# Mixer C's units of a hybrid encoder: other PSUM banks, other queueing, and A's outputs transposed at other jobs

## The chip, the cores and the metric

The kernel runs on one core of a Trainium2 chip. The metric is device microseconds of that core. One execution of the kernel before was also profiled; its times below come from that one.

## The reference, cut to what matters

Two layers work on 256 tokens of width 1024. Per layer, one projection of the normalised input gives queries, keys and values of four attention mixers A, B, C, D, and four gates. Each mixer's output goes through its own branch matrix, is gated, and the sum goes through an output matrix; then a gated feed-forward part with a three-tap convolution follows.

```python
aq, ak, av, bq, bk, bv, cq, ck, cv, dq, dk, dv, g = split_parts(h @ w_in[l])
o_a = diff_attention(aq, ak, av, lam[l], subln_g[l], lambda_init)   # 4 heads, two softmaxes each, then RMSNorm
o_c = dilated_attention(cq, ck, cv)   # 8 heads; windows with dilations 1, 4, 16, joined by their denominators
merged = sum(gate[:, :, i] * (o_i @ w_branch[l, i]))    # i over A, B, C, D
x = x + merged @ w_out[l]
x = x + conv_ffn(rms_norm(x, norm2_g[l]), ...)
```

## The kernel before, in words

**Jobs.** All large matrices stream through the core as jobs. A job is 1 MB of weights: it is loaded (three jobs ahead), each half is split into a high part (`hi`, a cast on ACT, L281) and a low part (`lo`, a subtraction on DVE, L285), and PE multiplies with three passes: high by high (L338), low weights by high (L339), high weights by low (L340). A job of a projection is 24 products of 128 x 512. `ORDER` lists the projections of a layer: `qA` is the queries of mixer A, `gA0` the first half of gate A, `bA0` the first half of A's branch matrix, and so on. A projection of 1024 rows takes two jobs, a branch half one.

**Attention units.** Between the products of the jobs stand the attention units. `UNITS` gives for each mixer the job at which its first unit is handed in and the distance of the next ones (C: job 37, then every 1.5 jobs). A unit of C is two heads of one tile of 128 queries; there are 4 for each of 2 tiles. `go(i)` hands in, at one point, the steps of three neighbouring units: the transposes of unit i-1's probabilities (`transp`, L542, each followed by a copy to SBUF on ACT, L647), the multiplication of unit i-2's probabilities by the values (`pv`, L538) and unit i's scores (`score`, L538). The scores of C are two whole-array matmuls for each head (the dense window) and eight 64 x 64 ones (the dilated groups). Mask and row minimum run on DVE (L576), the exponential on ACT (L577), the reciprocal on DVE (L579), the scaling on ACT (L582).

**Order.** Within the handed-in program a list scheduler with its own timeline decides in which order the instructions stand on each engine, subject to data, buffers and explicit edges: `behind` puts an instruction behind named ones. `mma` and `tra` chain a unit's PE instructions one behind the other, through `self.chain`, which is empty at the start of a `go`. `self.last_mm` is the last product of a job so far. On each engine the instructions run in the order in which they stand.

**PSUM.** Eight banks: four under the tag `mm` for products, three under `ts` for transposes and scores, one under `o`. C's outputs of a tile's four units gather in the `o` bank (L701 in `pv`) and leave it at once after the last unit (`evac_split`: a cast on ACT, L442, then a subtraction on DVE, L448).

**A's outputs.** `finish` scales and normalises A's outputs of a tile (DVE L719, ACT L721 for squares, DVE L723, two POOL instructions, DVE L725). `o_transpose` (L737) transposes them and splits them into two tiles of its own from `o_tiles`; it is handed in one job before `bA0`. The tiles `qs` hold the queries of a mixer, split into a high and a low part; they are free once the last scores are done. Mixer B already writes its outputs there.

Of the kernel before, what the change touches and what calls it, by code (L numbers as in the profile page):

```python
# [11 lines left out]
F32R = mybir.dt.float32r  # L12
# [5 lines left out]
S = 256  # L18
# [64 lines left out]

UNITS = {MD: (11, 1.75), MB: (9.75, 1.1), MA: (22.75, 1.1), MC: (37, 1.5)}


class Trunk:
# [465 lines left out]

    def score(self, u):

# [4 lines left out]
        if m == MC:  # L560

            ps, es = [self.ps("ts") for i in range(2)], [self.etile() for i in range(2)]
            u["e"] = es
            self.dense_score(ps[0][:, :256], st, 2 * k, t)
            for g in (1, 2):
                for b in range(2):
                    bs = slice(t * 128 + 64 * b, t * 128 + 64 * b + 64)
                    c0 = 256 + 64 * ((g - 1) if b == 0 else (2 - g))
                    for i in (1, 0):
                        r = slice(64 * i, 64 * i + 64)  # L570
                        self.mma(ps[i][64 * b:64 * b + 64, c0:c0 + 64], st["qT"][g][r, k, bs], st["kT"][g][r, k, bs], start=True, stop=True)
            self.dense_score(ps[1][:, :256], st, 2 * k + 1, t)
            mn = self.small("mn", 8)
# [75 lines left out]
    def pv(self, u):  # L649
# [33 lines left out]
        if m == MD:  # L683
# [7 lines left out]
            w = lambda x: x.rearrange("p k (u t s j) -> p t s k u j", u=4, t=2, s=2)[:, t]  # L691
            oh, ol = (w(x) for x in self.o_tiles(st))
            self.evac_split([(pv[:, s], oh[:, s], ol[:, s]) for s in range(2)])
            return
        if k == 0:
            st["o"] = self.ps("o")
        o = st["o"]
        for i in range(3):
            for b in range(1 if i < 2 else 2):

                w = slice(0, 128) if i < 2 else slice(64 * b, 64 * b + 64)  # L701
                for a in range(2):
                    hs = slice((2 * k + a) * 64, (2 * k + a) * 64 + 64)
                    self.mma(o[64 * a:64 * a + 64, k * 128 + w.start:k * 128 + w.stop], v[0][:, i, hs] if i < 2 else v[1 + t][:, b, hs],
                             u["pt"][a][:, i * 128 + w.start:i * 128 + w.stop], start=i == 0, stop=i == 2 and b == 1)
        if u["last"]:
            self.evac_split([(four(o), *(half(x, t) for x in self.o_tiles(st)))])

# [17 lines left out]

    def o_tiles(self, st):
        if "oT" not in st:
            st["oT"] = [self.t4([128, 4, S], F32R) for i in range(2)]
        return st["oT"]  # L730

    def o_transpose(self, st, m, t):
        if m != MA:
            return
        p = self.ps("ts")
        for i in range(4):
            self.nc.tensor.transpose(p[:, i * 128:(i + 1) * 128], st["osb"][:, t, i * 128:(i + 1) * 128], self.ident)  # L737
        self.evac_split([(four(p), *(half(x, t) for x in self.o_tiles(st)))], scale=st["scale"][:, 0:1])


    def layer(self, l):
# [182 lines left out]
        def units(m, s0, step):  # L924
# [5 lines left out]
            def go(i):  # L930
                self.chain = None
                steps = ((i - 1, lambda u: self.transp(u, 0)), (i - 2, self.pv), (i - 1, lambda u: self.transp(u, 1)), (i, self.score))
                for j, f in steps:
                    if 0 <= j < len(us):
                        f(us[j])

# [8 lines left out]
        for what in ORDER.split():  # L945
# [10 lines left out]
            elif kind == "v":  # L956
                vblock(i, (AV, None, CV, DV)[i] + c * 512, c)
            elif kind == "g":
                gate(i, c)
                if i not in seen:  # L960
                    for t in range(2):
                        self.at(J(slot[0] - 1), t, lambda i=i, t=t: self.o_transpose(stt[i], i, t))
            else:
                branch(i, c, seen <= {i})
# [6 lines left out]
        for i, (s0, step) in UNITS.items():  # L971
            units(i, s0, step)
        ns = slot[0]

# [326 lines left out]
```

## Time and profile before

| | |
|---|---|
| median of 3 runs (lowest to highest) | 1230.11 us (1229.86 to 1231.45) |
| the profiled execution's own time | 1229.92 us |
| its span | 1228.1 us |
| PE busy | 1205.8 us, 98% |
| DVE, ACT, POOL busy | 889.7, 729.9, 124.2 us |

Times in the profile run from the span's start. A line such as L338 is a line of the kernel before; PE is the matrix engine, DVE the vector engine, ACT the scalar engine. The span starts a little after the execution's begin and ends a little before its end, so 1.8 us lie around it.

### The profile page before, as it was taken

What the parts mean: (1) busy time and instruction counts of PE and PEld (TensorE: products, weight loads), DVE (VectorE), ACT (ScalarE), POOL (GpSimd) and SP (SyncE); (2) the same over time, 40 slices, a digit from 0 to 9 for tenths busy, and PEclk for the clock granted to TensorE, in tenths of its full rate; (3) what the DMA queues carried; (4) which work ended last, traced back from release to release, by engine and by line L of the source; (5) the groups of instructions that cost most, each with busy time, mean ns of one, the idle gap of its engine ahead of it and who ended that gap; (6) DMA issues with size and microseconds to landing.
All of it is one profiled execution on the core that took longest, in us unless ns stands there. A gap on an engine that the chain in (4) does not pass through costs nothing.

```text
span 1228.1 us, 18650 instructions
## 1 busy us (share of the span) xinstructions
PE 1205.8 (98%) x7325; PEld 1031.0 (84%) x7325; DVE 889.7 (72%) x1431; ACT 729.9 (59%) x1219; POOL 124.2 (10%) x88
## 2 busy tenths in 40 slices
PE   8999999999899999999999999999998999999998
PEld 6887788888778899998878878788886888999986
DVE  6898876975446598886488978769664566888853
ACT  4557666566654466665365676755756545666641
POOL 0331130310000000000023202113000000000000
PEclk9999999999899999999999999999999999999999
DMA  8757346544455465565544754556353453655651
GB/s 261 247 166 234 122 161 199 172 171 144 148 140 172 137 201 178 178 217 175 203 169 157 208 187 142 172 167 204 106 184 110 147 196 104 235 178 173 199 180 66
DMA packets 127670, 212.08 MB, mean 173 GB/s; under 512 B 9085, under 2 KB 56797, under 8 KB 127582
## 3 DMA queue, kind: packets, MB, share of 16 engines
q1 hardware_dynamic: 125836, 205.90, 50.5%
q0 software_dynamic: 1280, 4.20, 1.5%
q8 instruction: 58, 0.95, 0.3%
q10 hardware_dynamic: 466, 0.79, 0.2%
q14 instruction: 30, 0.25, 0.1%
HBM read 203.53 MB, written 1.05 MB: 167 GB/s over the span
## 4 chain that ended last, share of the span: by engine, by line
PE 94%; ACT 3%; DVE 2%; DMA 0%; issue 0%; POOL 0%; SPq 0%; DVEq 0%; ACTq 0%; POOLq 0%
PE mm L338 18%; PE mm L340 18%; PE mm L339 18%; PE mm L336 7%; PE mm L335 7%; PE mm L334 7%; PE ts L538 3%; PE ts L340 2%; PE ts L339 2%; PE ts L338 2%; PE o L538 2%; PE ts L542 2%; PE ts L508 1%; PE o L340 1%; PE o L338 1%; PE o L339 1%
## 5 line engine op out<-in xcount | busy, mean ns | idle before, releaser
L285 DVE TENSOR_TENSOR lo<-w,hi 128x1024 fp32r<-128x1024 f32 x376 | 456.8, 1223 | 207.9 <-ACT hi L281 207.0
L281 ACT CAST hi<-w 128x1024 fp32r<-128x1024 f32 x376 | 392.6, 1049 | 296.4 <-PE mm L340 171.7
L338 PE MATMUL mm<-hi,hTh 128*128 128x512 f32 (+1 forms) x796 | 310.4, 391 | 1.7 <-DVE qn L495 0.5
L339 PE MATMUL mm<-lo,hTh 128*128 128x512 f32 (+1 forms) x796 | 308.6, 388 | 0.4 <-DVE lo L285 0.4
L340 PE MATMUL mm<-hi,hTl 128*128 128x512 f32 (+1 forms) x796 | 307.3, 388 | 0.0
L336 PE MATMUL mm<-hTl,hi 128*128 128x256 f32 x672 | 190.2, 283 | 0.0
L335 PE MATMUL mm<-hTh,lo 128*128 128x256 f32 x672 | 190.2, 283 | 0.0
L334 PE MATMUL mm<-hTh,hi 128*128 128x256 f32 x672 | 189.9, 283 | 0.0
L338 PEld LDWEIGHTS mm<-hi,hTh 128*128 128x128 f32 x796 | 149.7, 188 | 34.4 <-issue 2.2
L339 PEld LDWEIGHTS mm<-lo,hTh 128*128 128x128 f32 x796 | 149.7, 188 | 30.3 <-issue 1.5
L340 PEld LDWEIGHTS mm<-hi,hTl 128*128 128x128 f32 x796 | 149.7, 188 | 29.9 <-DVE hTl L448 0.9
L336 PEld LDWEIGHTS mm<-hTl,hi 128*128 128x128 f32 x672 | 129.1, 192 | 0.0
L335 PEld LDWEIGHTS mm<-hTh,lo 128*128 128x128 f32 x672 | 129.1, 192 | 0.0
L334 PEld LDWEIGHTS mm<-hTh,hi 128*128 128x128 f32 x672 | 128.9, 192 | 0.0
L338 PE MATMUL mm<-hi,t 128*128 128x512 f32 (+1 forms) x192 | 74.2, 387 | 4.1 <-ACT t L442 4.1
L160 POOL TENSOR_TENSOR sm_qr<-sm_qr,mhalf 128x16 f32<-128x16 f32 (+1 forms) x24 | 77.5, 3228 | 2.0
L340 PE MATMUL mm<-hi,t 128*128 128x512 f32 (+1 forms) x192 | 73.6, 384 | 0.0
L339 PE MATMUL mm<-lo,t 128*128 128x512 f32 (+1 forms) x192 | 73.3, 382 | 0.0
L1103 ACT ACTIVATE e<-mm,cwT 128x256 f32<-128x256 f32 x88 | 47.1, 561 | 30.9 <-PE mm L336 29.8
L406 POOL TENSOR_TENSOR sm_nr<-sm_nr,mhalf 128x1 f32<-128x1 f32 x8 | 4.4, 550 | 502.6 <-DVE sm_nr L403 493.8
L159 POOL TENSOR_SCALAR sm_qr<-sm_qr 128x16 f32<-128x16 f32 (+1 forms) x24 | 25.7, 1073 | 283.1 <-DVE sm_qr L497 283.0
L538 PE MATMUL ts<-t,t 64*64 64x64 f32 (+2 forms) x576 | 51.9, 274 | 0.3
(164 smaller groups left out, 1603.5 us busy)
## 6 DMA issues: line engine op xcount, KB each, us to landing
w<-in_w_in_dram SPq DMA_DIRECT2D x97, 1024.0 KB, 4.9
w<-in_w_up_dram SPq DMA_DIRECT2D x44, 1024.0 KB, 4.9
w<-in_w_down_dram SPq DMA_DIRECT2D x22, 1024.0 KB, 4.8
w<-in_w_branch_dram SPq DMA_DIRECT2D x16, 1024.0 KB, 4.9
w<-in_w_out_dram SPq DMA_DIRECT2D x8, 1024.0 KB, 4.9
t<-t POOLq DMA_DIRECT2D x16, 256.0 KB, 4.7
t<-t SPq DMA_DIRECT2D x32, 64.0 KB, 2.0
t<-in_rpb_dram SPq DMA_DIRECT2D x32, 62.5 KB, 5.1
```

The source lines that it names most:

```text
L159: nc.gpsimd.tensor_scalar(dst, ss, EPS, None, op0=ALU.add)
L160: nc.gpsimd.tensor_tensor(dst, dst, mh, ALU.pow)
L281: self.nc.scalar.copy(hi, w)
L285: self.last_split = self.nc.vector.tensor_tensor(lo, w, hi[:].bitcast(F32), ALU.subtract).ins
L334: mm(out, wh, xh, start=first, stop=False)
L335: mm(out, wl, xh, start=False, stop=False)
L336: mm(out, wh, xl, start=False, stop=last)
L338: mm(out, xh, wh, start=first, stop=False)
L339: mm(out, xh, wl, start=False, stop=False)
L340: self.last_mm = mm(out, xl, wh, start=False, stop=last).ins
L538: self.chain = (self.nc.tensor.matmul(out, stationary, moving, **kw).ins,)
L1103: nc.scalar.activation(y[:, b:b + 256], o[:, b:b + 256], AF.Identity, scale=cw(1, z), bias=cw(3, z))
```

## The change

1. `score` for C takes two banks of which the second is the `o` bank. The first (`u["bank"]`) is a `ts` bank that unit i shares with the outputs of unit i-2: scores in columns 0 to 383, outputs in 384 to 511. The 64 x 64 scores come first, then the dense ones.
2. `pv` of C returns a function that splits the unit's outputs; it is called behind the next scores. The outputs go to the place of C's queries (`qs`), unit by unit.
3. `go` starts its chain at `self.last_mm`, and hands in the two transposes first, then the multiplication, then the scores.
4. A's outputs are transposed at jobs 33 and 38 (`OUT_A`) and written to the place of A's queries. `o_tiles` is gone; only D keeps output tiles of its own.

On PE, in layer 1, where the kernel before scores its fifth unit of C and then transposes it: `ts` and `o` are PSUM banks, `e` probabilities, `pt` transposed probabilities. Before:

```order
L538 MATMUL ts_2990<-t_497_2548,t_473_2414 64x64
L538 MATMUL ts_2989<-t_497_2548,t_473_2414 64x64
L538 MATMUL ts_2990<-t_328_1735,t_448_2284 128x256
L538 MATMUL ts_2990<-t_330_1737,t_448_2284 128x256
L542 MATMUL ts_3069<-ident,e_2991 128x128 x3
L538 MATMUL o_2770<-pt_2969,t_400_2068 64x128
L538 MATMUL o_2770<-pt_2983,t_400_2068 64x128
```

The transposes of `e_2991` stand directly behind the last scores of the same unit. After (its line numbers are higher by 2 to 7; L341 to L343 are the three products), at a unit of C:

```order
L342 MATMUL mm_3358<-lo_3268,hTh 128x512
L343 MATMUL mm_3358<-hi_3267,hTl 128x512
L341 MATMUL mm_3359<-hi_3267,hTh 128x512
L342 MATMUL mm_3359<-lo_3268,hTh 128x512
L545 MATMUL ts_3194<-ident,e_3110 128x128 x3
L545 MATMUL ts_3200<-ident,e_3111 128x128 x3
L541 MATMUL ts_3193<-pt_3090,t_400_2068 64x128
L541 MATMUL ts_3193<-pt_3096,t_400_2068 64x128
L541 MATMUL ts_3193<-pt_3090,t_400_2068 64x128
```

The six transposes stand behind 37 products counted from the unit before, and the multiplication follows both groups.

On PE, at A's output transposes of layer 1 (`t_408_2099` holds A's normalised outputs). Before, tile 0, in front of the first products of A's branch matrix:

```order
L538 MATMUL ts_3094<-t_328_1735,t_448_2284 128x256
L538 MATMUL ts_3094<-t_330_1737,t_448_2284 128x256
L737 MATMUL ts_3176<-ident,t_408_2099 128x128 x4
L338 MATMUL mm_3269<-hi_3148,t_626_3181 128x512
L339 MATMUL mm_3269<-lo_3149,t_626_3181 128x512
L542 MATMUL ts_3185<-ident,e_3095 128x128 x3
```

After, tile 0, between A's last multiplication (`o_2229`) and the head transposes of C (L511):

```order
L343 MATMUL mm_2593<-hi_2588,hTl 128x512
L541 MATMUL o_2229<-t_242_1301,pt_2310 128x128 x4
L739 MATMUL ts_2427<-ident,t_408_2099 128x128 x4
L511 MATMUL ts_2556<-ident,qn_2481 128x128 x4
L511 MATMUL ts_2562<-ident,qn_2481 128x128 x4
L341 MATMUL mm_2736<-hi_2632,hTh 128x512
L342 MATMUL mm_2736<-lo_2633,hTh 128x512
```

The branch products that read the result come some ten jobs later; those of `mm_2736` that now follow the head transposes are of another projection.

On ACT, at the same place (`mm_2496`, `mm_2497`, `mm_2503`, `mm_2504` are product banks with C's values). Before:

```order
L281 CAST hi_2736<-w_2641 128x1024
L532 COPY t_497_2548<-ts_2549 128x4x128
L838 COPY t_500_2573<-mm_2496 64x512 x2
L838 COPY t_501_2574<-mm_2497 64x512 x2
L838 COPY t_500_2573<-mm_2585 64x512
L721 ACTIVATE o_2229<-t_408_2099 128x512
L838 COPY t_500_2573<-mm_2585 64x512
```

After:

```order
L284 CAST hi_2750<-w_2648 128x1024
L445 ACTIVATE t_231_1232<-ts_2427,sg_163 128x4x128
L728 ACTIVATE o_2229<-t_408_2099 128x512
L535 COPY t_498_2555<-ts_2556 128x4x128
L840 COPY t_501_2580<-mm_2503 64x512 x2
L840 COPY t_502_2581<-mm_2504 64x512 x2
L840 COPY t_501_2580<-mm_2592 64x512 x2
```

The copy of A's transposed outputs (L445) is new there, and the squares of `finish` (L721, now L728) moved from behind five copies of C's values to in front of them.

```diff
--- before.py
+++ after.py
@@ -82,6 +82,9 @@
 ORDER = "qD kB kD qB kA vD qA vA gD0 kC1 kC0 qC1 bD0 gD1 vC0 qC0 qC2 bD1 kC2 vC1 vC2 gB0 bB0 gB1 bB1 gA0 bA0 gA1 bA1 gC0 bC0 gC1 bC1"
 
 UNITS = {MD: (11, 1.75), MB: (9.75, 1.1), MA: (22.75, 1.1), MC: (37, 1.5)}
+
+
+OUT_A = (33, 38)
 
 
 class Trunk:
@@ -551,7 +554,7 @@
     def etile(self):
         return self.sb(self.tp, "e", [128, 512], F32, bufs=4)
 
-    def score(self, u):
+    def score(self, u, out=None):
 
         nc = self.nc
         m, t, k, st = u["m"], u["t"], u["k"], u["st"]
@@ -559,9 +562,8 @@
         st["sums"][t] = sums
         if m == MC:
 
-            ps, es = [self.ps("ts") for i in range(2)], [self.etile() for i in range(2)]
+            ps, es = [u.get("bank") or self.ps("ts"), self.ps("o")], [self.etile() for i in range(2)]
             u["e"] = es
-            self.dense_score(ps[0][:, :256], st, 2 * k, t)
             for g in (1, 2):
                 for b in range(2):
                     bs = slice(t * 128 + 64 * b, t * 128 + 64 * b + 64)
@@ -569,7 +571,10 @@
                     for i in (1, 0):
                         r = slice(64 * i, 64 * i + 64)
                         self.mma(ps[i][64 * b:64 * b + 64, c0:c0 + 64], st["qT"][g][r, k, bs], st["kT"][g][r, k, bs], start=True, stop=True)
-            self.dense_score(ps[1][:, :256], st, 2 * k + 1, t)
+            for i in range(2):
+                self.dense_score(ps[i][:, :256], st, 2 * k + i, t)
+            if out:
+                out()
             mn = self.small("mn", 8)
             for i in range(2):
                 e, h = es[i][:, :384], 2 * k + i
@@ -689,22 +694,24 @@
                         self.mma(o[64 * a:64 * a + 64, c], v[1 + t][:, s, h * 64:h * 64 + 64], u["pt"][a][:, c], start=True, stop=True)
             pv = o.rearrange("p (k s u j) -> p s k u j", k=4, s=2, u=4)
             w = lambda x: x.rearrange("p k (u t s j) -> p t s k u j", u=4, t=2, s=2)[:, t]
-            oh, ol = (w(x) for x in self.o_tiles(st))
+            if t == 0:
+                st["oT"] = [self.t4([128, 4, S], F32R) for i in range(2)]
+            oh, ol = (w(x) for x in st["oT"])
             self.evac_split([(pv[:, s], oh[:, s], ol[:, s]) for s in range(2)])
             return
-        if k == 0:
-            st["o"] = self.ps("o")
-        o = st["o"]
+
+        o = u.get("bank") or self.ps("ts")
         for i in range(3):
             for b in range(1 if i < 2 else 2):
 
                 w = slice(0, 128) if i < 2 else slice(64 * b, 64 * b + 64)
                 for a in range(2):
                     hs = slice((2 * k + a) * 64, (2 * k + a) * 64 + 64)
-                    self.mma(o[64 * a:64 * a + 64, k * 128 + w.start:k * 128 + w.stop], v[0][:, i, hs] if i < 2 else v[1 + t][:, b, hs],
+                    self.mma(o[64 * a:64 * a + 64, 384 + w.start:384 + w.stop], v[0][:, i, hs] if i < 2 else v[1 + t][:, b, hs],
                              u["pt"][a][:, i * 128 + w.start:i * 128 + w.stop], start=i == 0, stop=i == 2 and b == 1)
-        if u["last"]:
-            self.evac_split([(four(o), *(half(x, t) for x in self.o_tiles(st)))])
+
+        st["oT"] = st["qs"]
+        return lambda: self.evac_split([(o[:, 384:], *(half(x, t)[:, k] for x in st["oT"]))])
 
     def finish(self, u, o):
 
@@ -724,18 +731,13 @@
         self.rsqrt_mean(rr[:, :4], rr[:, :4], 4)
         nc.vector.tensor_tensor(hv(osb), hv(osb), rr.unsqueeze(2).to_broadcast([128, 4, 128]), ALU.mult)
 
-    def o_tiles(self, st):
-        if "oT" not in st:
-            st["oT"] = [self.t4([128, 4, S], F32R) for i in range(2)]
-        return st["oT"]
-
-    def o_transpose(self, st, m, t):
-        if m != MA:
-            return
+    def o_transpose(self, st, t):
+
+        st["oT"] = st["qs"]
         p = self.ps("ts")
         for i in range(4):
             self.nc.tensor.transpose(p[:, i * 128:(i + 1) * 128], st["osb"][:, t, i * 128:(i + 1) * 128], self.ident)
-        self.evac_split([(four(p), *(half(x, t) for x in self.o_tiles(st)))], scale=st["scale"][:, 0:1])
+        self.evac_split([(four(p), *(half(x, t) for x in st["oT"]))], scale=st["scale"][:, 0:1])
 
 
     def layer(self, l):
@@ -928,11 +930,20 @@
             us = [{"m": m, "t": t, "k": k, "st": stt[m], "l": l, "last": k == n - 1} for t in range(2) for k in range(n)]
 
             def go(i):
-                self.chain = None
-                steps = ((i - 1, lambda u: self.transp(u, 0)), (i - 2, self.pv), (i - 1, lambda u: self.transp(u, 1)), (i, self.score))
-                for j, f in steps:
-                    if 0 <= j < len(us):
-                        f(us[j])
+
+                self.chain = (self.last_mm,)
+                out = None
+                if m == MC and 2 <= i < len(us):
+                    us[i - 2]["bank"] = us[i]["bank"] = self.ps("ts")
+                if 1 <= i <= len(us):
+                    for j in range(2):
+                        self.transp(us[i - 1], j)
+                if i >= 2:
+                    out = self.pv(us[i - 2])
+                if i < len(us):
+                    self.score(us[i], out)
+                elif out:
+                    out()
 
             for i in range(len(us) + 2):
                 self.fat(J(s0 + i * step), lambda i=i: go(i))
@@ -957,9 +968,6 @@
                 vblock(i, (AV, None, CV, DV)[i] + c * 512, c)
             elif kind == "g":
                 gate(i, c)
-                if i not in seen:
-                    for t in range(2):
-                        self.at(J(slot[0] - 1), t, lambda i=i, t=t: self.o_transpose(stt[i], i, t))
             else:
                 branch(i, c, seen <= {i})
             if kind == "b":
@@ -970,6 +978,8 @@
         self.at(J(20), -1, scale_a)
         for i, (s0, step) in UNITS.items():
             units(i, s0, step)
+        for t, j in enumerate(OUT_A):
+            self.at(J(j), 1, lambda t=t: self.o_transpose(stt[MA], t))
         ns = slot[0]
```

## Rows read from the trace of the kernel before

**Rows 1.** The page: engines (busy, share, instructions), and the chain's shares by engine.

```profile
PE 1205.8 (98%) x7325; PEld 1031.0 (84%) x7325; DVE 889.7 (72%) x1431; ACT 729.9 (59%) x1219; POOL 124.2 (10%) x88
...
PE 94%; ACT 3%; DVE 2%; DMA 0%; issue 0%; POOL 0%; SPq 0%; DVEq 0%; ACTq 0%; POOLq 0%
```

**Rows 2.** PE's waits over the run: total, times, longest, in us.

```profile
PE ts L542 <- ACT e L582: 5.3, 2, 2.6
PE mm L338 <- ACT t L442: 4.1, 4, 1.4
```

**Rows 3.** Stages: length, busy time by engine, granted clock (PEclk), DMA share, GB/s.

```profile
324.00:331.00 7.00, 4.21 (x49) 3.26 (x48) 3.24 (x7) 5.05 (x11) 0.00 (x0) 0.91 0.45 152
331.00:338.00 7.00, 5.88 (x47) 4.69 (x47) 2.22 (x7) 4.05 (x10) 0.00 (x0) 0.60 0.21 76
930.00:937.00 7.00, 4.21 (x52) 3.17 (x52) 2.79 (x7) 5.37 (x12) 0.00 (x0) 1.00 0.44 150
937.00:943.00 6.00, 4.60 (x45) 3.76 (x43) 2.45 (x7) 3.95 (x10) 0.00 (x0) 0.72 0.28 87
```

**Rows 4.** Timeline of PE, layer 1, 322 to 344: start, length, idle before.

```profile
322.39 0.39 PE L338 MATMUL mm<-hi,hTh 128*128 128x512 f32 x1
...
322.61 0.39 PE L339 MATMUL mm<-lo,hTh 128*128 128x512 f32 x1
...
325.11 0.49 PE L542 MATMUL ts<-ident,e 128*128 128x128 f32 x3
...
325.53 0.89 PE L538 MATMUL o<-pt,t 128*64 128x128 f32 x16
...
330.81 0.90 PE L542 MATMUL ts<-ident,e 128*128 128x128 f32 x3 [2.65 <-ACT e L582]
...
331.64 1.55 PE L538 MATMUL o<-pt,t 128*64 128x128 f32 x16
...
335.61 1.05 PE L737 MATMUL ts<-ident,t 128*128 128x128 f32 x4
...
337.79 0.50 PE L338 MATMUL mm<-hi,t 128*128 128x512 f32 x1 [1.12 <-ACT t L442]
...
338.13 0.40 PE L339 MATMUL mm<-lo,t 128*128 128x512 f32 x1
...
343.43 0.60 PE L737 MATMUL ts<-ident,t 128*128 128x128 f32 x4
```

**Rows 5.** Timeline of PE and ACT, layer 1, 269 to 275.

```profile
269.90 1.04 PE L508 MATMUL ts<-ident,qn 128*128 128x128 f32 x8
...
270.69 0.48 PE L340 MATMUL mm<-hi,hTl 128*128 128x512 f32 x1
...
271.89 1.04 PE L508 MATMUL ts<-ident,qn 128*128 128x128 f32 x8
...
272.69 1.38 PE L538 MATMUL ts<-t,t 128*128 128x256 f32 x20
...
273.01 2.97 ACT L838 COPY t<-mm 64x512 f32<-64x512 f32 x5
...
274.24 0.50 PE L338 MATMUL mm<-hi,hTh 128*128 128x512 f32 x1 [0.17 <-ACT t L838]
```

**Rows 6.** Timeline of DVE and ACT, a softmax of C, layer 1.

```profile
342.06 0.56 DVE L576 CUSTOM_DVE_ANT_0 e<-ts,maskc 128x384 f32<-128x384 f32 x1 [3.54 <-PE ts L538]
...
344.65 1.11 ACT L582 ACTIVATE e<-e,sm_cf 128x384 f32<-128x384 f32 x2
```

**Rows 7.** Groups by line: busy, mean ns; idle before, who released it.

```profile
L281 ACT CAST hi<-w 128x1024 fp32r<-128x1024 f32 x376 | 392.6, 1049 | 296.4 <-PE mm L340 171.7 <-PE o L340 58.6 <-PE mm L336 48.5
...
L448 DVE TENSOR_TENSOR t<-o,t 128x256 fp32r<-128x256 f32 (+1 forms) x20 | 9.1, 472 | 9.1 <-ACT t L442 9.1
...
L442 ACT CAST t<-o 128x256 fp32r<-128x256 f32 (+1 forms) x20 | 7.9, 419 | 2.1 <-PE o L538 2.1
...
L442 ACT ACTIVATE t<-ts,sg 128x512 fp32r<-128x512 f32 x4 | 2.7, 677 | 0.2
```

## The prediction

> **What bounds the kernel now.** I read the page's engine shares and its chain first. The matrix engine PE is busy for 98% of the span and carries 94% of the chain [rows 1]. So only two things can shorten the run: time in which PE waits or runs slowly, and time that PE loses when it changes between kinds of work. Vector (DVE, 72%) and scalar (ACT, 59%) matter only where PE waits for them.
>
> The list of PE's waits comes next. Two sorts lie where the change works [rows 2]. The transposes of mixer C's probabilities wait for the softmax, 5.3 us in 2 waits. The first products of A's branch matrix wait for the copies of A's transposed outputs, 4.1 us in 4 waits. Both occur once in each layer's stage, at 324 to 345 us and at 930 to 950 us.
>
> The table by stage then shows a second loss at the same place: the granted clock. It is 0.91 in 324 to 331 us and 0.60 in 331 to 338 us, so 0.09 x 2 x 7 + 0.40 x 2 x 7 = 6.9 us passed at 1.2 GHz instead of 2.4. In layer 2 it is 1.00 and then 0.72 of 6 us, so 3.4 us [rows 3]. Before it fell, PE had stood idle for 2.65 us in either layer (5.3 over 2).
>
> The timeline shows why [rows 4]. At 325.11 a C unit is transposed and its successor multiplied and scored, all without products between. The next transposes need the softmax of the unit just scored and start only at 330.81. From there on the same groups take 0.90 instead of 0.49 us (three transposes), 1.55 instead of 0.89 (16 passes of probabilities by values) and 1.05 instead of 0.60 (A's four transposes). A's transposes start at 335.61, and the first product on their result at 337.79.
>
> **The change part by part, in us over both layers.**
>
> 1. *C's units queued behind products.* In the order after, 31 to 41 products stand between one unit's scores and its transposes; before, two units of a layer had none or two. The 5.3 of waiting goes. What is late next is the softmax itself. At 342.06 its first reduction starts and its second scaling ends at 344.65 + 1.11 = 345.76 [rows 6], a chain of 3.7 us. The cover is at least 31 x 0.23 (322.39 to 322.61 is one product's pitch [rows 4]) = 7 us, mostly 8.4. With one high-part cast of 1.05 in ACT's way [rows 7] and one low part on DVE of the same order, the chain is some 6 us. I take no wait.
>
> 2. *A's outputs transposed at jobs 33 and 38.* Their first reader is now some ten jobs away. The 4.1 goes.
>
> 3. *Tails of those six waits.* A wait is counted from the end of the last pass, but PE normally starts the next before that: transposes that began at 269.90 end at 270.94, and the product behind them starts at 270.69 [rows 5], 0.25 earlier. So 6 x 0.25 = 1.5 more.
>
> 4. *The half clock.* The three pairs of groups above sum to 3.50 against 1.98, a factor of 1.77. The work from 330.81 to 336.66 (5.85 us) would have taken 3.3, a loss of 2.5. Layer 2's 3.4 us by the same factor lose 1.5. Sum 4.0, gone with the wait that precedes it.
>
> 5. *Fewer changes of kind.* Counting in both orders, between the same two places of a layer, each step from one kind of PE work to another (products, transposes, whole-array scores, 64 x 64 scores, probabilities by values): 71 before, 54 after. One change costs about 0.11: the product at 337.79 is followed after 0.34 [rows 4], not 0.23. 17 x 2 x 0.11 = 3.7. Bounds: 0, if the skipped changes are the cheap ones, and 7, if each costs twice that.
>
> 6. *The new wait.* This is the dear part. A's first transposes (tile 0) now stand in front of C's head transposes, and on ACT their copy and the squares of A's normalisation (L721) stand in front of the copies L838 that free a product bank. Before, PE already waited there, 0.17 us at 274.24, for the second of those copies (they run from 273.01 at 0.6 each [rows 5]). After, 0.68 (A's copy [rows 7]) and 0.6 (the squares) come first, which puts the second copy's end at about 274.2 + 1.25 = 275.45. PE is there sooner, because the scores that it did at 272.69 now come behind those products. From 271.89 it has A's 4 and 8 head transposes; 8 took 0.80 there from start to start (to 272.69), so 12 take 1.2 and it could go on at 273.1. It stands 2.3, and the 0.17 with its tail of 0.25 is gone: 2 x (2.3 - 0.4) = 3.8 added. Bounds: 0 (ACT catches up) and 3.0 a layer (one more cast in front).
>
> 7. *The clock after the new wait.* The rows have the clock fall after gaps of 2.65 and not after one of 1.1 (335.61 + 1.05 to 337.79; at 343.43 A's transposes take 0.60 again [rows 4]). The new gap is 2.3 less a tail, 2.1, nearer to 2.65, so I let it fall once in each layer, at the price of layer 2's stretch: 2 x 1.5 = 3.0. Bounds 0 and 5. The Trainium skill, in "TensorE: Matmul & The Clock Gate" (HAM oscillation), lets the clock drop only after idle gaps longer than any of these. By that rule this term is 0 and the sum 3.0 lower; the trace does not agree, as 2.65 was enough.
>
> 8. *Evacuations unit by unit.* C's outputs leave in 8 pieces of 128 x 128 a layer instead of 2 of 128 x 512, so 12 more copies on ACT and 12 more subtractions on DVE over the run. A 128 x 256 piece takes 0.42 and 0.47 [rows 7]; smaller ones no more. That is 5.0 and 5.7 us at most on engines that are busy for 59 and 72% [rows 1], so nothing on PE. Without that cover they delay a softmax by 0.9, inside the 1 to 2.4 us that term 1 leaves. The wait that the shared bank adds (the outputs leave after the next scores) holds up only that copy and the mask behind it.
>
> 9. *The end.* The last unit's outputs are multiplied later, during gate C and its branch product. The order has the products of the next gate step in front of those that need them: 17 to 20 products, 3.9 us, behind the multiplication, against 0.9 for copy and subtraction. No wait. Nothing changes from the first merge transposes on. The new tile places (four fewer tiles a layer) take away waits of loads, if anything, and no PE wait is on a load there.
>
> **Sum.** Removed 5.3 + 4.1 + 1.5 + 4.0 + 3.7 = 18.6; added 3.8 + 3.0 = 6.8; net 11.8 less. The profiled execution took 1229.92 us (span 1228.1), so 1218.1, and since the median of the runs shown is 1230.11, 0.2 higher, 1218.3 for a median. I say 1218.3.
>
> **Rivals.**
>
> *The clock holds through the new gap, or the gap does not come.* For it: 2.1 is short of every gap after which it fell, and the rule of the skill above. Against: 2.65 is near. Time 1215.3 with the gap alone, 1211.5 without either.
>
> *Waits come back elsewhere.* PE asks for weights some 1% sooner, and ACT and DVE get 24 more instructions. For it: DVE is already busy for 72% [rows 1]. Against: ACT's casts wait for PE (171.7 of 296.4 us idle [rows 7]), so ACT is ahead. If half of the removed 18.6 returns: 1227.6.
>
> *Slower: the softmax is later than its cover in every unit.* One place, C's transposes in the unit after the scores, where 3 + 3 now stand in front of everything else, so that nothing of the unit runs while they wait. Before, the multiplication of the unit two back stood between them. Worst case of the chain: 3.7, two casts (2.1) and two low parts (2.4) in the way, and the shared bank's copy and subtraction first (0.9), 9.1 in all against 7 to 9.4 of cover. It decides from an overrun of 11.8 / 14 = 0.85 us a unit on; at 1.7 a unit PE loses 24 and the time is 1242. Against: casts wait for PE, and no two stand side by side in more than a few units. The Trainium skill, in "PSUM — Partial Sum Buffer" (Terms, PSUM bank), forbids two engines in one bank at once, so a bank that holds outputs and scores makes copy, subtraction and mask take turns; that is the 0.9 above. No run here shows it, since before each had its own bank.
>
> *The change does not do what it says.* The order shows that it does, in both layers alike, so I give this no chance of its own.
>
> **How the numbers follow.** The forecast, a gain of 9 to 15 us with the new wait: 0.62. Clock or gap milder, a gain over 13: 0.22. Half of it back, with a net gain of 0 to 6: 0.10, of which 0.04 within 0.2%. Slower: 0.06. The likeliest case alone spans 1215 to 1221 (terms 5 to 7). The range takes in 1211.5 below and most of the half-way case above: 1211 to 1225. With 0.2% (2.5 us) as what a measurement can tell from no change: faster 0.90, same 0.04, slower 0.06.
>
> **What would show it.** Right: no wait of C's transposes on L582 nor of a branch product on L442 in the list of waits; a granted clock of 1.00 over what was 324 to 345; a new wait of 2 us of a product on the L838 copy, once a layer, at about 275.5 and 870, with a clock under 1.00 right behind it. Wrong: that wait under 1 us or over 3; waits of C's transposes in many units; a span over 1225.

## The result and the profile after

The kernel after takes 1216.55 us (median of 4, 1215.56 to 1220.21) against 1230.78 (median of 4, 1229.86 to 1232.05) on the same chip: a ratio of 0.9889, 95% interval 0.9865 to 0.9913. The forecast was 1218.3, in a range from 1211 to 1225. The profiled execution is the longest of the four, 1220.21 us with a span of 1218.4.

Two lines of its page, the engines' busy times and the chain by engine, answer to [rows 1]:

```profile
PE 1202.7 (99%) x7325; PEld 1032.1 (85%) x7325; DVE 891.3 (73%) x1443; ACT 730.1 (60%) x1231; POOL 123.3 (10%) x88
...
PE 96%; ACT 2%; DVE 1%; DMA 0%; issue 0%; SPq 0%; POOL 0%; ACTq 0%; DVEq 0%; POOLq 0%
```

PE is still the bound, now for 99% of the span. The first lines of the list of PE's waits after, which answer to [rows 2] (engine, tile and line that waited, releaser: us in total, times, longest):

```profile
PE mm L341 <- ACT t L840: 3.9, 2, 2.0
PE ts L1232 <- DMA t<-in_norm_g_dram: 2.3, 1, 2.3
PE o L429 <- DVE t L414: 1.4, 1, 1.4
```

Both waits that the change was expected to remove are gone (L542 and L442 of before are L545 and L445 here), and one is new: a product waits for the second copy of C's values (L840, before L838). The other two lines belong to the start and to the step between the layers.

The table by stage for the whole stretch that differs, in before: the first row is layer 1, the second layer 2. (Stretch, its length, busy us of PE, PEld, DVE, ACT and POOL with instructions, granted clock, DMA share, GB/s.) Here and in every run below it begins and ends at the same products, the first ahead of C's first scores, the last behind C's outputs.

```profile
266.97:407.17 140.20, 135.34 (x842) 110.17 (x840) 76.70 (x112) 83.43 (x135) 1.27 (x2) 0.98 0.50 161
873.42:1012.84 139.42, 134.28 (x842) 109.44 (x840) 76.31 (x113) 83.13 (x135) 1.27 (x2) 0.99 0.46 156
```

The same two stretches after, then what was the place of the half clock [rows 3], then the two places behind the new wait:

```profile
268.35:402.59 134.24, 132.27 (x842) 109.45 (x840) 77.40 (x118) 83.18 (x141) 1.27 (x2) 0.99 0.52 168
868.84:1002.99 134.15, 132.18 (x842) 109.33 (x840) 76.79 (x119) 83.11 (x141) 1.27 (x2) 0.99 0.49 162
...
320.00:345.00 25.00, 25.00 (x174) 20.81 (x173) 15.35 (x27) 15.76 (x28) 0.00 (x0) 1.00 0.74 210
...
276.80:280.30 3.50, 3.50 (x9) 2.67 (x9) 0.69 (x1) 3.42 (x7) 1.12 (x2) 0.51 0.00 0
...
877.50:881.00 3.50, 3.50 (x25) 2.49 (x25) 0.83 (x2) 2.87 (x5) 0.09 (x1) 0.51 0.00 0
```

The layers gain 140.20 - 134.24 = 5.96 and 139.42 - 134.15 = 5.27, together 11.2. Between 320 and 345 us PE is now busy throughout at full clock, and the half clock has moved to 3.4 us behind the new wait in each layer. The span is only 9.7 shorter, because this execution began the stretch 1.4 later (268.35 against 266.97): ahead of it both kernels do the same, and other executions of one and the same PE order began it between 266.66 and 268.52. What differs there is shown with the repeated run below. So a difference of 2 us between medians can be the start, and the stretches are the finer measure.

The timeline of PE after, at a C unit (answers to [rows 4]) and at the new wait (answers to [rows 5]; start, us, engine, line, [idle before <- releaser]):

```profile
271.28 1.04 PE L511 MATMUL ts<-ident,qn 128*128 128x128 f32 x8
272.07 0.48 PE L343 MATMUL mm<-hi,hTl 128*128 128x512 f32 x1
272.39 1.05 PE L541 MATMUL o<-t,pt 128*128 128x128 f32 x8
273.28 0.60 PE L739 MATMUL ts<-ident,t 128*128 128x128 f32 x4
273.71 1.04 PE L511 MATMUL ts<-ident,qn 128*128 128x128 f32 x8
276.71 0.74 PE L341 MATMUL mm<-hi,hTh 128*128 128x512 f32 x1 [1.97 <-ACT t L840]
...
322.90 0.82 PE L545 MATMUL ts<-ident,e 128*128 128x128 f32 x6
323.64 0.89 PE L541 MATMUL ts<-pt,t 128*64 128x128 f32 x16
325.19 0.40 PE L541 MATMUL o<-t,t 128*128 128x256 f32 x2
```

And ACT at the new wait:

```profile
272.92 1.07 ACT L284 CAST hi<-w 128x1024 fp32r<-128x1024 f32 x1
273.91 0.69 ACT L445 ACTIVATE t<-ts,sg 128x512 fp32r<-128x512 f32 x1
274.50 0.59 ACT L728 ACTIVATE o<-t 128x512 f32<-128x512 f32 x1
275.02 0.59 ACT L535 COPY t<-ts 128x512 f32<-128x512 f32 x1
275.50 2.96 ACT L840 COPY t<-mm 64x512 f32<-64x512 f32 x5
```

PE has nothing to do from the end of the head transposes (273.71 on) to 276.71, and ACT has A's copy (L445) and squares (L728) in front of the copies of C's values. The unit's transposes at 322.90 wait for nothing.

### The profile page after: what moved, and what is told of

It reads as the page before. It is cut to its first block, busy times and chain, and to the rows that moved or that the text cites. A ratio compares the mean times of both kernels' runs of the same rounds, so it can differ in the third digit from the quotient of the medians.

```text
span 1218.4 us, 18690 instructions
## 1 busy us (share of the span) xinstructions
PE 1202.7 (99%) x7325; PEld 1032.1 (85%) x7325; DVE 891.3 (73%) x1443; ACT 730.1 (60%) x1231; POOL 123.3 (10%) x88
## 3 DMA queue, kind: packets, MB, share of 16 engines
HBM read 203.53 MB, written 1.05 MB: 168 GB/s over the span
## 4 chain that ended last, share of the span: by engine, by line
PE 96%; ACT 2%; DVE 1%; DMA 0%; issue 0%; SPq 0%; POOL 0%; ACTq 0%; DVEq 0%; POOLq 0%
PE mm L341 18%; PE mm L342 18%; PE mm L343 18%; PE mm L339 7%; PE mm L338 7%; PE mm L337 7%; PE ts L541 3%; PE ts L341 2%; PE ts L343 2%; PE ts L342 2%; PE o L541 2%; PE ts L545 2%; PE ts L511 1%; PE o L343 1%; PE o L341 1%; PE o L342 1%
## 5 line engine op out<-in xcount | busy, mean ns | idle before, releaser
L341 PE MATMUL mm<-hi,hTh 128*128 128x512 f32 (+1 forms) x796 | 311.4, 392 | 5.4 <-ACT t L840 3.9
L343 PE MATMUL mm<-hi,hTl 128*128 128x512 f32 (+1 forms) x796 | 308.3, 389 | 0.0
L341 PEld LDWEIGHTS mm<-hi,hTh 128*128 128x128 f32 x796 | 150.1, 189 | 38.1 <-ACT t L840 4.4
L343 PEld LDWEIGHTS mm<-hi,hTl 128*128 128x128 f32 x796 | 150.1, 189 | 29.9 <-DVE hTl L451 0.9
L341 PE MATMUL mm<-hi,t 128*128 128x512 f32 (+1 forms) x192 | 73.9, 385 | 0.0
L343 PE MATMUL mm<-hi,t 128*128 128x512 f32 (+1 forms) x192 | 72.9, 381 | 0.0
L1114 DVE SCALAR_TENSOR_TENSOR e<-mm,cwT,e 128x255 f32<-128x255 f32 x88 | 39.7, 478 | 17.0 <-ACT e L1113 17.0
```

The lines of the kernel that those rows point to most:

```text
L341: mm(out, xh, wh, start=first, stop=False)
L343: self.last_mm = mm(out, xl, wh, start=False, stop=last).ins
L1114: nc.vector.scalar_tensor_tensor(y[:, b + 1:b + 256], o[:, b:b + 255], cw(0, z), y[:, b + 1:b + 256], op0=ALU.mult, op1=ALU.add)
```

## The experiments

All times are medians with the interval of the ratio to the kernel before, each against before on its own chip (1230.4 for the first eight, 1231.85 for the last three). "Stretch" is layer 1's stretch between the same products as above.

The question was which edit removes the softmax wait. Step 1 of the prediction gave it to C's edits. But in PE's order with A's part alone C's units also stand apart, so I set T1 against T2.

**A's part alone** (the kernel before, and):

```
+        st["oT"] = st["qs"]
...
-                if i not in seen:
-                    for t in range(2):
-                        self.at(J(slot[0] - 1), t, lambda i=i, t=t: self.o_transpose(stt[i], i, t))
...
+        for t, j in enumerate((33, 38)):
+            self.at(J(j), 1, lambda t=t: self.o_transpose(stt[MA], t))
```

> The kernel before with one part of the change alone: A's outputs transposed at jobs 33 and 38 into the place of its queries; C's units as before. T1 (the prediction's steps 1 and 2): each part takes away its own wait, so only the wait on A's copies (4.1 us) goes, the wait of C's transposes on the softmax (5.3 us in 2) and the clock's fall behind it stay, and the new wait on the L838 copies is added: 1226 to 1231 us. T2 (rival, from the order of this kernel, in which 34 to 44 products now stand between C's units although C's code is untouched): the early transposes are what spreads C's units; both waits and the old half clock go, and the new wait comes: about 1219 to 1221, the kernel after plus its 15 spared changes of kind a layer, 15 x 2 x 0.11 = 3.3 us.

Measured: 1226.59 us, 0.9954 to 0.9979; stretch 137.92. Its list of waits, its stretch, and its timeline of PE at the end of C:

```profile
PE ts L542 <- ACT e L582: 6.2, 2, 3.1
...
PE mm L338 <- ACT t L442: 1.4, 2, 0.7
...
266.81:404.73 137.92, 133.22 (x841) 109.14 (x840) 76.14 (x112) 83.20 (x135) 1.27 (x2) 0.99 0.51 163
```

```profile
372.08 0.90 PE L538 MATMUL ts<-t,t 64*64 64x64 f32 x18
376.08 0.55 PE L542 MATMUL ts<-ident,e 128*128 128x128 f32 x3 [3.10 <-ACT e L582]
376.55 1.50 PE L538 MATMUL o<-pt,t 128*64 128x128 f32 x16
...
381.42 0.50 PE L338 MATMUL mm<-hi,t 128*128 128x512 f32 x1 [0.69 <-ACT t L442]
```

The time is T1's, but not for T1's reason: the softmax wait has moved from 330 us to the last two units at 376, and 3.4 us at 1.2 GHz follow it there (the 16 passes take 1.50 instead of 0.89). The wait on L442 that is left is not on A's copies: at 381.42 a product waits for the cast of C's own outputs, which the same line of code makes.

**C's part alone** (the kernel after, with A's transposes back at the job ahead of bA0):

```
+                if i == MA and c == 0:
+                    for t in range(2):
+                        self.at(J(slot[0] - 1), t, lambda t=t: self.o_transpose(stt[MA], t))
...
-        for t, j in enumerate(OUT_A):
-            self.at(J(j), 1, lambda t=t: self.o_transpose(stt[MA], t))
```

> The kernel after without A's part: A's outputs are transposed again right before their branch products. T1: C's units are queued behind products by their own edits, so the wait of C's transposes on the softmax (5.3 us) and the half clock behind it go, the wait on A's copies (4.1) stays, no new wait on L838: 1217 to 1221 us. T2: C's units bunch again (two of them with no product between), so the softmax wait and the half clock stay beside the wait on A's copies, and only the spared changes of kind (71 to 51 a layer, 20 x 2 x 0.11 = 4.4 us) are won: about 1226.

Measured: 1234.38 us, 1.0018 to 1.0043, slower than before; stretch 141.98.

```profile
PE ts L545 <- ACT e L587: 6.4, 2, 3.2
PE mm L341 <- ACT t L445: 5.1, 4, 1.8
PE mm L341 <- ACT t L840: 2.6, 2, 1.3
```

```profile
338.56 0.50 PE L341 MATMUL mm<-hi,t 128*128 128x512 f32 x1 [1.80 <-ACT t L445]
...
339.30:342.60 3.30, 3.26 (x8) 2.58 (x9) 0.06 (x1) 1.12 (x2) 0.00 (x0) 0.50 0.06 18
```

T1 falls: with all of C's edits the softmax wait is there, in the middle of C as before. T2 had the waits right and the sign of the time wrong: the three waits are together 14.1 us against 9.7 in before (5.3, 4.1 and 0.3 on L838), and in each layer the clock falls a second time, behind the wait on A's copies. By the stretches (141.98 against 140.20, and 141.95 against 139.42 in layer 2) this is more than the spared changes give back.

**Without the ordering edge**:

```
-                self.chain = (self.last_mm,)
+                self.chain = None
```

> The kernel after without the ordering edge from the last product to a unit (chain = None). T1: that edge is what queues C's units behind products; without it they bunch and the softmax wait and half clock return: 1224 to 1228 us. T2: the edge changes next to nothing in PE's order, so the time is that of the kernel after within 0.2%: 1215 to 1219, with the same list of waits.

Measured: 1217.46 us, 0.9875 to 0.9907. PE's order is that of after, instruction by instruction, and so is the list of waits: T2 holds, and this edge, a part of the third edit, does nothing here. The run tells more by its clock:

```profile
268.52:401.19 132.67, 130.70 (x841) 108.32 (x840) 77.41 (x118) 83.12 (x141) 1.27 (x2) 1.00 0.54 170
...
867.48:1000.16 132.68, 130.71 (x841) 108.32 (x840) 76.80 (x119) 83.06 (x141) 1.27 (x2) 1.00 0.49 164
...
276.80:280.30 3.50, 3.41 (x30) 2.69 (x31) 0.91 (x2) 3.40 (x7) 1.27 (x2) 1.00 0.00 0
```

```profile
276.89 0.50 PE L341 MATMUL mm<-hi,hTh 128*128 128x512 f32 x1 [1.97 <-ACT t L840]
```

The same idle 1.97 us, and the clock stays at 2.4 GHz. That prices a fall: 134.24 - 132.67 = 1.57 in layer 1, 134.15 - 132.68 = 1.47 in layer 2.

**Which of C's edits.** Neither part alone removes the wait, so a new pair: T3 (banks) against T4 (order of steps). Old steps in the kernel after:

```
-                    for j in range(2):
-                        self.transp(us[i - 1], j)
+                    self.transp(us[i - 1], 0)
                 if i >= 2:
                     out = self.pv(us[i - 2])
+                if 1 <= i <= len(us):
+                    self.transp(us[i - 1], 1)
```

> The kernel after with the old order of steps within a unit (first transposes, values, second transposes, scores); banks, units' places and A's part stay. The run with A's part alone kept a softmax wait at the end of C, where two units stand side by side, so what is left of C's part must remove it. T3 (banks): a unit that takes two banks for its scores passes some 40 products instead of 52, so C ends while products are still left; the order of steps is no matter. Then there is no wait on the softmax here, and only 9 more changes of kind a layer: 18 x 0.06 to 0.11 = 1.1 to 2.0 us, so 1217.5 to 1218.5. T4 (steps): transposes in one piece before the values are what parts the units; then the softmax wait of 5 to 6 us is back: 1221 or more.

Measured: 1220.70 us, 0.9904 to 0.9934; stretch 134.10 at a clock of 1.00.

```profile
266.91:401.01 134.10, 132.13 (x842) 108.37 (x841) 77.13 (x118) 83.60 (x141) 1.27 (x2) 1.00 0.53 168
```

No softmax wait, the new wait as after; the 9 changes a layer cost 134.10 - 132.67 = 1.43, more than expected. The profiled execution, at 1218.39, lies in T3's range; the median lies 2.2 above it, and whether that is the start or a fall of the clock in the other executions (up to 1221.93) is not shown. And the new steps with before's banks and A's part:

```
-  steps = ((i - 1, lambda u: self.transp(u, 0)), (i - 2, self.pv), (i - 1, lambda u: self.transp(u, 1)), ...
+  steps = ((i - 1, lambda u: self.transp(u, 0)), (i - 1, lambda u: self.transp(u, 1)), (i - 2, self.pv), ...
```

> The kernel before with A's part and the new order of steps, but each unit still with two rotating banks for scores and a third for outputs kept over four units. T3 (banks): the units still take 52 products each, the last two stand side by side and the softmax wait (6.2 us in the run with A's part alone) stays; 6 changes of kind a layer are spared, 12 x 0.06 to 0.11 = 0.7 to 1.3: 1225 to 1226. T4 (steps): no softmax wait, 1219 to 1221.

Measured: 1228.03 us, 0.9970 to 0.9988; stretch 138.24, with

```profile
PE ts L542 <- ACT e L582: 6.2, 2, 3.1
...
267.09:405.33 138.24, 133.55 (x841) 109.13 (x840) 76.38 (x112) 82.62 (x135) 1.27 (x2) 0.99 0.50 163
```

Both go T3's way: the order of steps neither brings the wait nor takes it away; that the 6 spared changes a layer saved nothing was not expected by either. T3 says banks, but what is left of C's part holds also the order of the scores and the outputs that leave unit by unit, and no run takes these apart. In PE's order it can be seen where products are missing (P: products with their number, T: transposes, V: values, B and D: 64 x 64 and whole-array scores), at the end of C:

```
A's part alone   D P10 B D P42 T V T D P10 B D P34 T V T D P6 B D T V T   (two units side by side)
C's part alone   B D P41 T V B D P33 T V B D T V B D T4 P12 T V B D       (side by side ahead of bA0)
after            B D P41 T V B D P37 T V B D P37 T V B D P37 T P20 V B D P40 T
```

From C's first scores to its eighth, layer 1 passes 348 products with A's part alone, under either order of steps, and 281 after; that a unit which needs fewer rotating banks is let in sooner is how I read this, not something a run shows by itself. In the first row the next product in line behind the last two units is one of C's branch matrix, which waits for the units' own outputs (the 0.69 at 381.42). In the second it is one of A's branch matrix, which waits for A's transposes, and these stand behind C's units (the 1.80 at 338.56). In both rows gate products, which read only the normalised input, stand a little later (from 381.99 and 347.77): products exist, but none stands where it would cover the softmax, and whether the scheduler could have put them there no run shows. Among all the runs only those with both edits have no such place.

**The new wait.** A's transposes at other jobs, in the kernel after:

```
-OUT_A = (33, 38)
+OUT_A = (40, 42)
```

In another run it is (32, 38).

> The kernel after with A's outputs transposed at jobs 40 and 42 instead of 33 and 38. On ACT the copies of C's values then stand in front of A's squares again. Prediction's steps 6 and 7: the new wait on L838 (3.9 us in 2) goes and with it the clock's fall behind it (0 to 3 us); A's copies still have time before their first reader. So 1210 to 1213 us against 1216.5. Rival: the time in the new wait was PE being early, and it waits elsewhere instead: 1216 to 1218.

Measured: 1217.62 us, 0.9880 to 0.9910; stretch 133.56.

```profile
PE mm L341 <- ACT t L840: 2.6, 2, 1.3
...
PE mm L341 <- DVE gates L921: 1.6, 2, 0.8
```

> The kernel after with the first of A's two output transposes one job earlier (32 instead of 33). In PE's order C's first scores then stand again between the head transposes and the products that wait for the copies of C's values, as before. The wait on L840 (2.0 us a layer) should shrink to about the 0.9 that the scores waited in the run with A's part alone, where PE came to this place in the same order: 2.2 us less over both layers, and no cause for the clock to fall there (0 to 3 us): 1213 to 1215. Rival, as with jobs 40 and 42: PE comes early to the next wait, and nothing is won: 1216 to 1218.

Measured: 1215.94 us, 0.9871 to 0.9898; stretch 132.38.

```profile
PE o L541 <- DVE sm_rr L730: 2.7, 2, 1.3
```

Both misses, and both show what else holds this place. Without A's copy and squares in front 1.30 of 1.97 is left, and at a branch product at 393.03 PE is 0.8 early instead; four more transposes (0.4 us) also fall inside this stretch, so it is not the same work as the others. With C's scores ahead of the products, they wait for the bank "o", which A's last unit holds until its norm is done. The kernel after ran once more beside the latter.

> The kernel after once more, for comparison on the same chip. If the clock falls behind the new wait only in some executions, as the granted clocks of its runs (0.993 and 1.0) suggest, the times lie in two groups some 3 us apart, the executions with the lower clock above: median 1216 to 1217.5. If the 3 us between its runs have another cause, the times don't go with the clock.

Measured: 1215.95 us, 0.9872 to 0.9899. The profiled execution kept the clock behind the wait, with a stretch of 132.67 as without the edge. The times don't form two groups by the clock: 1215.70 came at a mean of 1.0 and 1215.50 at 0.998, with the highest, 1217.18, at 0.996. What the start is can be seen ahead of the first full job. The first line is the run without the edge, whose stretch began at 268.52, the second the run with jobs 34 and 39 below, whose stretch began at 266.87:

```profile
13.40 1.05 PE L364 MATMUL mm<-hi,hTl 128*128 128x512 f32 x2
...
11.59 0.63 PE L364 MATMUL mm<-hi,hTl 128*128 128x512 f32 x2
```

In the three profiled executions that began the stretch at 268.35 or later such pairs take 1.05 us up to about 16 us; in the ten others (266.66 to 267.15) for half as long or not at all. So the start is itself a matter of TensorE's rate, and the mean clock does not tell it apart from a fall behind the new wait: it is 1.0 for the run without the edge in spite of its slow start, and the 0.998 of this run's profile lies at the start, not at the wait. Of executions without a profile neither part is known.

**Both score banks of C's first unit from "ts"**:

```
-            ps, es = [u.get("bank") or self.ps("ts"), self.ps("o")], ...
+            ps, es = [u.get("bank") or self.ps("ts"), self.ps("o" if t or k else "ts")], ...
```

> The same with A's outputs transposed at jobs 40 and 42, so that neither A's copy and squares nor the later place of C's scores is left at this spot. If these two are the whole of the new wait on L840 (1.3 us a layer is left of 2.0 with 40 and 42 alone), it should be 0.2 a layer as in the kernel before, and the time that of jobs 40 and 42 (1217.62) less 2 x 1.3: 1215. The wait on the gates (0.8 a layer) stays. If the wait has another cause, it stays at 1.3 a layer and the time at 1217.5.

Measured: 1213.98 us, 0.9835 to 0.9867. The stretch is 130.97 us, of which PE is busy for all:

```profile
268.79:399.76 130.97, 130.97 (x842) 108.65 (x840) 77.29 (x118) 82.83 (x140) 1.27 (x2) 1.00 0.53 171
```

```profile
273.71 1.04 PE L511 MATMUL ts<-ident,qn 128*128 128x128 f32 x8
274.68 1.44 PE L541 MATMUL ts<-t,t 64*64 64x64 f32 x20
276.06 0.50 PE L341 MATMUL mm<-hi,hTh 128*128 128x512 f32 x1
```

The scores fill the 1.3, and the wait on the gates that I expected to stay is gone too.

> The kernel after (1215.95 us in the last comparison) with two edits: C's first unit takes both its score banks from the rotation ts, so that its scores need not wait for the bank o that A's last unit holds, and A's outputs are transposed at jobs 34 and 39. In PE's order C's first scores stand behind the 12 transposes and ahead of the products, as in the run with A's part alone, where the gap was 1.18 us from start to start against 2.24 in the kernel after. If the new wait is a cost of its own, 2 x 1.06 = 2.1 us go: 1213.8. If PE only comes early to its next wait, 1215.5 to 1216.5.

Measured: 1213.94 us, 0.9840 to 0.9870; stretch 131.77, so 0.90 less than after at full clock (132.67), against 1.06 expected.

> The kernel after with the first edit alone (both score banks of C's first unit from ts; jobs 33 and 38 stay). The gap shrinks by 1.06 a layer as above, but the order now cuts the second unit's 64 x 64 scores in two around 8 products, 2 more changes of tile shape a layer. At 0.16 to 0.18 each (2.86 us for 18 in the run with the old steps) that costs 0.6 to 0.7 over both layers: 1216 - 2.1 + 0.7 = 1214.5. If such a change costs nothing, 1213.8; if the gap is not won, 1216.5.

Measured: 1216.01 us, 0.9857 to 0.9886; stretch 132.31. The gap was won, and 0.54 of it is lost again against the run before. Two changes of shape more stand in the order where the scores are cut in two; A's transposes also stand one job earlier than there, so the 0.54 is not theirs alone for certain. The median is 1.5 above the expectation, which the stretch doesn't show; the starts vary by as much.

The version with jobs 40 and 42 and this edit beats both kernels by the stretches: 1.70 and 1.68 us below the kernel after at full clock (130.97 and 131.00 against 132.67 and 132.68), 3.27 and 3.15 below its profiled execution. The medians, 1213.98 and 1216.55, were not taken beside each other.

## Why the prediction was right, step by step

The time was 1.75 us under the forecast and on its side, with its main terms; one reason was wrong, one price was misread, and one event was taken as certain that is not.

1. *The softmax wait goes:* yes, 5.3 to none, and the cover holds: after, a unit's first reduction starts at 314.04 on DVE and its second scaling ends at 319.05 on ACT, 3.85 us ahead of its transposes at 322.90:

```profile
314.04 0.55 DVE L581 CUSTOM_DVE_ANT_0 e<-ts,maskc 128x384 f32<-128x384 f32 x1
...
317.93 1.12 ACT L587 ACTIVATE e<-e,sm_cf 128x384 f32<-128x384 f32 x2
```

The reason was wrong. "C's units queued behind products" needs products at that place, and that takes A's early transposes as well as C's edits; either part alone has 6.2 to 6.4 us of this wait. That the term came out is luck in so far as both edits stood in the one change. I read the whole order and credited one part with what only both do.

2. *The wait on A's copies goes:* yes, 4.1 to none. A's part does it: none is left with it alone (the 1.4 on L442 in that list is C's outputs), 5.1 without it.

3. *Tails, 1.5:* not measured by themselves; the sum below closes to 0.3 with them, which does not show them, since the other terms are no surer than that.

4. *The half clock, 4.0:* gone from its place [rows 3], and the price of 1.5 for 3.4 us is confirmed by 1.57 and 1.47.

5. *Changes of kind, 3.7:* the mis-sized term. Old steps add 9 changes a layer and 1.43 us, 0.16 each, but 6 fewer changes in the other pair of runs saved nothing (138.24 against 137.92, both with 3.4 us at half clock over different work). What tells the two apart is the shape of the tile: the first pair differs by 8 changes between 128 x 128, 128 x 64 and 64 x 64 a layer (34 against 26), the second by none (32 and 32). So 0.18 for a change of shape. The Trainium skill says as much in "TensorEngine Tiling (Array Packing)" (Key Properties): another tiling mode, not merely another tile, drains TensorE. It gives no price, and I had not weighed it. The rows of before agree. Behind the product at 270.69 [rows 5] the next passes of the same shape start at 271.00:

```profile
271.00 1.05 PE L538 MATMUL o<-t,pt 128*128 128x128 f32 x8
```

From 269.90 to 271.00 PE does 8 transposes (0.11 each from start to start, as the four from 273.28 to 273.71 after) and a product (0.23), together 1.11: two changes of kind add nothing. But from 325.11 to 325.53 [rows 4] three transposes ahead of passes of 128 x 64 take 0.42, 0.09 more than by themselves, and that is only the near side of the change. The price that I took, 0.34 from 337.79 to 338.13 instead of 0.23, was misread: the product at 270.69 needs 0.31 to the next start too, but it starts that much sooner behind its transposes (8 in 0.79). Before has 34 such changes and after 26, so the term is 8 x 2 x 0.18 = 2.9.

6. *The new wait:* 1.97 idle a layer against 2.1 forecast, at 276.7 and 876.3 us, by both causes named. A's copy and squares make 0.67 of it (1.97 against 1.30), C's scores behind the products the other 1.30, which vanishes when they stand ahead again and both their banks are free. Removing both gives back 1.70 of the 1.97 a layer; moving A's transposes alone gives nothing (1217.62).

7. *The clock falls behind it, 3.0:* in the profiled execution, in both layers and at 3.04. Not as a rule: with the same 1.97 the clock held in the profiled executions without the edge, with old steps and of the repeated kernel. Behind idle times of 2.65 (before) and 3.1 to 3.2 (either part alone) it fell each time, and with C's part alone once more in each layer behind the idle 1.80 and 1.72 at A's copies, at 339.3 in layer 1. By the Trainium skill, "TensorE: Matmul & The Clock Gate" (HAM oscillation), it would hold behind all of these; the trace disagrees for each of the longer ones, for 1.80 and 1.72, and for one execution of four with 1.97.

8. and 9. *Evacuation by unit and the end, nothing:* no wait names either. The Trainium skill's rule that no two engines may be in one bank at once ("PSUM — Partial Sum Buffer", Terms, PSUM bank) showed no price on PE: its one wait inside the stretch after is the 2.0 on L840.

The sum, both layers: 5.3 + 4.1 + 1.5 + 4.0 + 2.9 - 3.8 = 14.0 less without falls, and the stretches say (140.20 - 132.67) + (139.42 - 132.68) = 14.3. With two falls 11.0, measured 11.2. The medians, 14.2 apart, lie at the first, so the rival in which the clock holds (1215.3) describes most executions better than the forecast. Without falls the forecast's 11.8 is 3.0 too small by term 7 and 0.8 too large by term 5; the start, which moves a time by 2 us, hides as much. The rival in which waits come back elsewhere did not happen in this kernel, but it is what C's part alone does, and in part what jobs 40 and 42 did.

## What to carry to other kernels

When a unit's softmax is hidden behind another stream of work, ask at every place what keeps that stream supplied: two edits that each look complete can each only move the wait, and together remove it. Count PE's changes of tile shape, not its changes of operand, and take their price from start to start over both neighbours of the change. Compare stretches between the same instructions where medians differ by less than the start of the program varies.

## What the runs showed of the hardware

A change of tile shape on PE cost 0.18 us on the mean of 8 (1.43 us a layer); a change between transposes and products of the whole array cost nothing that can be seen (1.10 us for 8 transposes and a product). Behind an idle time of 1.97 us the granted clock fell to 1.2 GHz in both layers in one of four profiled executions and in neither layer of the other three; behind 1.80 and 1.72, which follow a longer idle time by some 6 us, it fell too. What decides that is open. The start of one program varied by 2 us between executions, with the first products at half rate for longer in the late ones (1.05 us a pair against 0.63).
